# Experts sorted on the chip by token count, the last three with 64 slots and a stationary operand of heads and rests

## The chip, the cores and the metric

The kernel runs on one core of one Trainium2 chip. The metric is the device time of one execution in microseconds; several executions are timed, and their median is quoted. The core's engines are TensorE (PE, matrix products; its loads of the stationary operand are shown apart, as PEld), VectorE (DVE), ScalarE (ACT), GpSimd (POOL) and SyncE (SP, which only issues transfers here). They run side by side and meet through semaphores. Each runs its own instructions in the order in which they were laid down when the kernel was built.

## The reference

Two decoder layers on x of 256 tokens by 1024 channels, in float32. Each layer adds a mixer (gated DeltaNet heads, forgetting attention, pooling) and then a feed-forward: a dense SwiGLU in the first layer, and in the second the top 2 of 8 experts. The change lies in that last part:

```python
N_EXPERTS, TOP_K, D_FF_EXPERT = 8, 2, 1536

def moe_swiglu(h, router, w_gate, w_up, w_down):
    probs = jax.nn.softmax(ht @ router, axis=-1)          # ht: [256, 1024]
    top_p, top_i = lax.top_k(probs, TOP_K)
    top_p = top_p / jnp.sum(top_p, axis=-1, keepdims=True)
    gates = jnp.sum(one_hot(top_i, N_EXPERTS) * top_p[..., None], axis=1)
    for e in range(N_EXPERTS):
        out = out + gates[:, e:e + 1] * swiglu(ht, w_gate[e], w_up[e], w_down[e])

def swiglu(h, w_gate, w_up, w_down):
    return (jax.nn.silu(h @ w_gate) * (h @ w_up)) @ w_down
```

With the inputs of this case the router gives experts 0 to 7 the token counts 58, 74, 57, 74, 68, 67, 62 and 52 (256 tokens, two experts each).

## The kernel before

Four phases follow one another: mixer 0, the dense feed-forward, mixer 1, and "all", the experts. Float32 products are made of reduced ones: each operand is split into a head (hi) and a rest (lo = value - hi), and three products hi hi + hi lo + lo hi are summed in PSUM (`mm3`, L240 and on; all products are recorded at the line of `mm`, L236).

The weights stream from HBM in pieces of 128 rows by at most 1152 columns, into a ring of 6 buffers, 12 in the experts' phase (`load`, L260; SP issues all of them, at L266). `piece` (L269) splits each: ACT copies the head into `whi` (recorded at L230), DVE subtracts, `wlo = raw - whi` (recorded at L233). There are four buffers of whi and four of wlo. Pieces have a high priority, so that they run ahead of the work around them.

`route` (L963) computes logits, the softmax, the two best experts, and each token's slot at its experts (`pos`). `experts` (L1063) then takes the eight experts in order of their numbers, each with 128 slots, each in four chunks of 384 hidden channels, 32 steps in all:

- `gather` (L1066), for two experts at a time: 32 products with a one-hot matrix (`disp`, filled by DVE at L1041) put the chosen tokens into `ghi` and `glo`, channels on partitions.
- `gate_up` (L1083): six pieces (1152, 1152 and 768 columns for the gate, the same for the up product). The tokens are the stationary operand and the weights are the moving one, 384 columns; 16 row tiles by three products make 48 matmuls into `ps_e`. ACT then makes `esg` (SiLU), and DVE multiplies `ehh = up * esg`.
- `down` (L1101), one step later: three transposes of `ehh` into `ps_ht`, a split into `ehi` and `elo`, and three pieces of 1024 columns. Three pieces by two halves by three products make 18 matmuls of 512 columns into `ps_y`.
- `finish` (L1115) scales and splits the result (`yh`, `yl`) and builds the one-hot `Q`; `scatter` (L1126), after every second expert, adds the rows back to `xs` with 16 matmuls (`ps_sc`) and four DVE additions.

A step has 9 pieces, 288 in the phase. The order in which instructions stand on each engine comes from a scheduler that plays the program through with its own estimates; the kernel sets only priorities. At the end the output is stored, and if an expert had more than 128 tokens, a second pass (L1193) does the rest.

Of the kernel before, what the change touches and what calls it, by code (L numbers as in the profile page):

```python
# [35 lines left out]
NFC = 4  # L36
EPS = 1e-6
# [3 lines left out]
# column groups of w_in, in the order they are streamed: name, columns, channels on partitions or not  # L41
# [12 lines left out]
# row tiles of w_out in the order they are streamed  # L54
# [25 lines left out]
def shape_constants():  # L80
# [30 lines left out]
    r.add("lt", np.broadcast_to((e[None, :] < e[:, None]).reshape(1, 64), (128, 64)))  # L111
    return c, r
# [25 lines left out]
def pack(inputs):  # L138
    """Lays the inputs out in the order the chip reads them."""
# [42 lines left out]
class Kernel:  # L182
# [101 lines left out]
    def hi_lo(self, hi, lo, src, scale=None):  # L284
        """hi = float32r(src * scale), lo = src * scale - hi; scale is one value per partition."""
        if scale is None:
            return self.copy(hi, src), self.tt(lo, src, hi.bitcast(F32), ALU.subtract)
# [26 lines left out]
    def rsqrt(self, out, v, n):  # L314
        """out = v ** -0.5: exp(-ln(v) / 2) with one Newton step."""
# [9 lines left out]
    def gain(self, i):  # L325
        """The i-th norm's gain, on every partition."""
# [45 lines left out]
    def proj_tokens(self, g, hi, lo):  # L372
        """[token, channel] products; psum tiles for both token tiles."""
# [12 lines left out]
    def proj_channels(self, g, hi, lo):  # L386
        """[channel, token] products, one psum tile of 128 channels after the other."""
# [10 lines left out]
    def gates(self, ps):  # L398
        """Log decays, betas and everything that follows from them alone."""
# [11 lines left out]
        # softplus(zz) = max(zz, 0) + log1p(exp(-|zz|)); log1p(y) = ln(u) + (y - (u - 1)) / u, u = 1 + y  # L411
# [71 lines left out]
    def scaled(self, ps):  # L483
        """A product with channels on partitions, times the norm's factors."""
# [4 lines left out]
    def conv(self, g, m, ps, dest):  # L489
        """Causal convolution over tokens and SiLU, channels on partitions."""  # L490
# [20 lines left out]
    def silu(self, dest, x, eng):  # L511
        """x / (1 + exp(-x)) = x exp(-ln(1 + exp(-x))), in the table of the other functions."""
# [7 lines left out]
    def rnorm(self, src, scale, tag, ps=None):  # L520
        """(sum over a head's channels of src**2 * scale + eps) ** -0.5, for [channel, token]."""
# [19 lines left out]
        # 16-blocks by substitution, one 32-block of N per partition  # L541
# [21 lines left out]
        # the entries that join two 16-blocks  # L563
# [3 lines left out]
        # keys times exp(G), and keys with tokens on partitions times exp(G_last - G) beta  # L567
        # exp(G_t) along the free dimension, for every channel of a head
# [494 lines left out]
    def experts(self, base, xh, xl):  # L1063
# [78 lines left out]
        for i in range(len(steps) + 1):  # L1142
            cur = None
            if i < len(steps):
                e, fc = steps[i]
                if i == 0:
# [4 lines left out]
                    if not base:  # L1151
                        self.gates_of_experts()
# [74 lines left out]
```

## Time and profile before

| | |
|---|---|
| runs | 1006.22, 1005.40, 1004.65 us; median 1005.4 us |
| profiled execution | 1006.0 us, of which the span of the page is all |
| busy over the span | PE 95%, PEld 86%, DVE 74%, ACT 64%, POOL 13% |
| chain that ended last | PE 81%, POOL 6%, DVE 6%, ACT 3%, DMA 2%, issue 2% |
| read from HBM | 222.48 MB, 222 GB/s over the span |

The busy shares are of the whole span; phases differ. The chain is followed back from the last instruction, at each step to whatever released it. Matmuls are pipelined: the duration of one is longer than its distance to the next, so rates are read from runs of them. DVE and ACT instructions overlap by a little in the same way.

### The profile page before, as it was taken

Reading aid. Unit: us, or ns where it says so; the run is one execution under the profiler, and the core shown is the slowest. Engines: PE = TensorE matmul, PEld = TensorE weight load, DVE = VectorE, ACT = ScalarE, POOL = GpSimd, SP = SyncE. Lnnn points to the kernel's source line nnn. Section 1 sums busy time; section 2 is a strip of 40 time slices with the busy share of each in tenths; the row PEclk is TensorE's granted clock in tenths of the full one; section 3 lists DMA queues with packets and bytes.
Section 4 is the critical chain, followed back from the end, with each engine's and each line's share of the span. In section 5 each row is a group of like instructions: output and inputs, shape, how many; then the busy total and the mean of one; then the engine's idle time right before and its main releaser. Section 6 shows DMA issues by size and latency. Waiting matters only on the chain.

```text
span 1006.0 us, 17495 instructions
## 1 busy us (share of the span) xinstructions
PE 955.4 (95%) x6715; PEld 868.7 (86%) x6715; DVE 746.9 (74%) x1013; ACT 642.4 (64%) x969; POOL 130.6 (13%) x196
## 2 busy tenths in 40 slices
PE   6988998999999989899985999999999999999997
PEld 6987877999999979888765999998999899998995
DVE  5876657655555578776566789888997899888995
ACT  6754646544444458556454688876888688886873
POOL 2596000000000024970002000000000000000000
PEclk9998999999999999999997999999999999999999
DMA  9534114666666545241162799998999899998981
GB/s 347 161 92 124 44 43 132 214 187 186 188 188 180 164 150 181 85 136 56 40 234 73 245 363 369 364 309 301 367 371 321 282 358 367 355 317 301 368 327 45
DMA packets 61979, 224.75 MB, mean 223 GB/s; under 512 B 6896, under 2 KB 7152, under 8 KB 61888
## 3 DMA queue, kind: packets, MB, share of 16 engines
q1 hardware_dynamic: 61344, 221.62, 64.2%
q0 software_dynamic: 544, 1.94, 0.6%
q8 instruction: 54, 0.88, 0.4%
q14 instruction: 37, 0.30, 0.1%
HBM read 222.48 MB, written 1.05 MB: 222 GB/s over the span
## 4 chain that ended last, share of the span: by engine, by line
PE 81%; POOL 6%; DVE 6%; ACT 3%; DMA 2%; issue 2%; SPq 0%; DVEq 0%; POOLq 0%; ACTq 0%
PE ps_e L236 26%; PE ps_y L236 13%; PE ps_gu L236 13%; PE ps_dn L236 6%; PE ps_out L236 4%; PE ps_fq L236 3%; DVE wlo L233 2%; PE ps_ga L236 2%; PE ps_zabf L236 2%; PE ps_o L236 1%; POOL cacc L500 1%; PE ps_p L236 1%; POOL U L562 1%; PE ps_ht L1104 1%; DVE cacc L504 1%
## 5 line engine op out<-in xcount | busy, mean ns | idle before, releaser
L233 DVE TENSOR_TENSOR wlo<-raw,whi 128x1024 fp32r<-128x1024 f32 (+3 forms) x418 | 501.0, 1223 | 133.8 <-ACT whi L230 130.4
L230 ACT ACTIVATE whi<-raw 128x1024 fp32r<-128x1024 f32 (+3 forms) x418 | 437.9, 1056 | 203.2 <-PE ps_e L236 57.9
L236 PE MATMUL ps_e<-wlo,ghi 128*128 128x384 f32 x512 | 173.1, 338 | 0.0
L236 PE MATMUL ps_e<-whi,glo 128*128 128x384 f32 x512 | 172.6, 338 | 0.0
L236 PE MATMUL ps_e<-whi,ghi 128*128 128x384 f32 x512 | 171.5, 340 | 0.0
L236 PE MATMUL ps_gu<-hThi,whi 128*128 128x256 f32 x352 | 99.8, 283 | 1.3 <-DVE hTlo L233 1.3
L236 PE MATMUL ps_gu<-hThi,wlo 128*128 128x256 f32 x352 | 99.4, 283 | 0.0
L236 PE MATMUL ps_gu<-hTlo,whi 128*128 128x256 f32 x352 | 99.4, 282 | 0.0
L236 PEld LDWEIGHTS ps_e<-wlo,ghi 128*128 128x128 f32 x512 | 97.2, 190 | 1.8
L236 PEld LDWEIGHTS ps_e<-whi,glo 128*128 128x128 f32 x512 | 97.0, 189 | 2.0
L236 PEld LDWEIGHTS ps_e<-whi,ghi 128*128 128x128 f32 x512 | 96.9, 190 | 0.9
L236 PE MATMUL ps_y<-wlo,ehi 128*128 128x512 f32 x192 | 75.5, 396 | 0.0
L236 PE MATMUL ps_y<-whi,elo 128*128 128x512 f32 x192 | 74.9, 396 | 0.0
L236 PEld LDWEIGHTS ps_gu<-hThi,whi 128*128 128x128 f32 x352 | 67.3, 191 | 2.5 <-DVE hTlo L233 1.5
L236 PEld LDWEIGHTS ps_gu<-hTlo,whi 128*128 128x128 f32 x352 | 67.3, 191 | 1.0
L236 PEld LDWEIGHTS ps_gu<-hThi,wlo 128*128 128x128 f32 x352 | 67.3, 191 | 0.0
L236 PE MATMUL ps_y<-whi,ehi 128*128 128x512 f32 x192 | 62.6, 397 | 1.7 <-ACT ehi L230 1.7
L236 PEld LDWEIGHTS ps_y<-whi,ehi 128*128 128x128 f32 x192 | 35.7, 188 | 8.6 <-ACT ehi L230 2.5
L236 PEld LDWEIGHTS ps_y<-wlo,ehi 128*128 128x128 f32 x192 | 36.1, 188 | 7.2
L236 PEld LDWEIGHTS ps_y<-whi,elo 128*128 128x128 f32 x192 | 35.8, 188 | 6.8 <-DVE elo L233 0.2
L236 PE MATMUL ps_dn<-whi,fhi 128*128 128x512 f32 x88 | 35.0, 398 | 0.0
L236 PE MATMUL ps_dn<-wlo,fhi 128*128 128x512 f32 x88 | 34.8, 396 | 0.0
(366 smaller groups left out, 1728.2 us busy)
## 6 DMA issues: line engine op xcount, KB each, us to landing
raw<-moe SPq DMA_DIRECT2D x128, 576.0 KB, 5.7
raw<-moe SPq DMA_DIRECT2D x96, 512.0 KB, 5.4
raw<-ffn SPq DMA_DIRECT2D x66, 512.0 KB, 3.6
raw<-moe SPq DMA_DIRECT2D x64, 384.0 KB, 5.4
raw<-win SPq DMA_DIRECT2D x34, 512.0 KB, 3.7
raw<-wout SPq DMA_DIRECT2D x16, 512.0 KB, 3.7
raw<-win SPq DMA_DIRECT2D x8, 402.0 KB, 5.1
raw<-win SPq DMA_DIRECT2D x4, 576.0 KB, 4.8
```

The lines of the kernel that those rows point to most:

```text
L230: return self.nc.scalar.activation(out, in_, AF.Copy, scale=scale)
L233: return self.nc.vector.tensor_tensor(out, a, b, op=op)
L236: self.nc.tensor.matmul(out, l, r, start=start, stop=stop)
L500: eng.tensor_scalar(acc, x, w[:, o + 3:o + 4], None, op0=ALU.mult)
L504: nc.vector.scalar_tensor_tensor(acc[:, j:], x[:, :T - j], wj, acc[:, j:], op0=ALU.mult, op1=ALU.add)
L562: nc.gpsimd.tensor_tensor(u, u, tv, op=ALU.subtract)
L1104: nc.tensor.transpose(ps[:, j * 128:j * 128 + 128], hh[:, j * 128:j * 128 + 128], self.ident)
```

## The change

Experts are given places. `places` sorts them by token count on DVE, most first (expert 0 always comes first, so that its weights can be streamed before the order is known), moves slots, gates and counts into that order, and SP reads the order into registers (`values_load_multi_w_load_instructions`); from the second place on, the address of each weight piece comes from such a register (`weights`). Gathers cover the places 0, 1-2, 3-4 and 5-7. The last three places have 64 slots: the stationary operand holds 64 columns of heads and 64 of rests, so two products (with whi and with wlo) take the place of three, and the two halves of the result are added, in `gate_up` by a copy on ACT and an addition on DVE for each of the two products. In `down` nothing is added: the halves go through `finish` as 128 rows, and the scatter sums them. In every `down`, small or not, the rest of the third piece is made by GpSimd instead of DVE. The second pass runs if one of the first five has more than 128 tokens or one of the last three more than 64.

```diff
+NL = 5
+    r.add("room", np.broadcast_to(np.where(e < NL, 0.0, 64.0), (128, 8)))
...
-    def piece(self, ap):
+    def piece(self, ap, eng=None):
...
-            parts = self.hi_lo(hi[:, :n], lo[:, :n], src)
+            parts = self.hi_lo(hi[:, :n], lo[:, :n], src, eng=eng)
...
+            return self.copy(hi, src), (eng or self.nc.vector).tensor_tensor(lo, src, hi.bitcast(F32), op=ALU.subtract)
...
+    def places(self):
+        nc.vector.tensor_copy(cnt, self.counts[:, 16:24])
+        nc.vector.tensor_copy(key, cnt)
+        nc.vector.memset(key[:, 0:1], 2.0 * T)
...
+        self.tt(c2, others, mine, ALU.is_equal)
+        self.tt(c1, others, mine, ALU.is_gt)
+        self.tt(c2, c2, self.rc("lt").rearrange("p (a b) -> p a b", b=NE), ALU.mult)
+        self.tt(c1, c1, c2, ALU.add)
+        nc.vector.tensor_reduce(place, c1, axis=AX.X, op=ALU.add)
...
+        nc.vector.tensor_copy(order, moved("orderf", self.rc("iota")[:, :NE]))
+        with self.tc.high_priority(offset=2 * AHEAD):
+            _, regs = nc.values_load_multi_w_load_instructions(order[0:1, 1:NE], engines=[mybir.EngineType.SP], min_val=0, max_val=NE - 1)
+        self.order = [0, *regs]
...
+        for o, v in ((by, self.pos), (gp, self.gate)):
+            self.tt(c4, at[:, None].to_broadcast([128, 2, NE, NE]), v[:, :, None, :].to_broadcast([128, 2, NE, NE]), ALU.mult)
+            nc.vector.tensor_reduce(o, c4, axis=AX.X, op=ALU.add)
...
+        groups = ((0, 2), (2, 4), (4, 6), (6, 8)) if over else ((0, 1), (1, 3), (3, NL), (NL, NE))
...
+        def gate_up(p, fc, g, e):
+            small = p >= nl
...
+                        if small:
+                            x = g[k // 4][:, k % 4, e]
+                            self.mm(ps[:, :384], x, wh[:, c], k == 0, False)
+                            self.mm(ps[:, :384], x, wl[:, c], False, k == 7)
+                        else:
+                            self.mm3(ps[:, :384], g[0][:, k, e], g[1][:, k, e], wh[:, c], wl[:, c], k == 0, k == 7)
...
+            if small:
+                for x, ps in zip((sg, hh), pgu):
+                    self.copy(x, ps[64:, :384])
+                    self.tt(x, ps[:64, :384], x, ALU.add)
+                ga, up = sg, hh
+            self.act(sg, ga, AF.Silu, scale=info[0][:r, p, 2:3])
+            self.tt(hh, up, sg, ALU.mult)
...
-                wh, wl = self.piece(self.d["moe"][e, fc, :, 2, j * D:(j + 1) * D])
+                wh, wl = self.piece(self.weights(p, fc, 2, j * D, j * D + D), nc.gpsimd if j == 2 else None)
...
+                    if small:
+                        x = h[:, j].rearrange("p i c -> p (i c)")
+                        self.mm(py[i], x, wh[:, c], first, False)
+                        self.mm(py[i], x, wl[:, c], False, last)
...
+                    fill(self.pos, *groups[0], 128)
+                    g[0] = gather(*groups[0])
+                    if not over:
+                        self.gates_of_experts()
+                        self.places()
+                    fill(self.pos, groups[0][1], nl, 128)
+                    if nl < NE:
+                        fill(self.pos, nl, NE, 64)
...
-                elif fc == NFC - 2 and e % 2 == 1 and e + 1 < NE:
-                    g[e // 2 + 1] = gather(e + 1)
+                elif fc == NFC - 2 and p + 1 < NE and of[p + 1] not in g:
+                    g[of[p + 1]] = gather(*groups[of[p + 1]])
...
+    def weights(self, p, fc, s, a, b):
+        e = self.order[p]
+        if p == 0:
+            return d[0, fc, :, s, a:b]
+        return d[bass.ds(e, 1), fc, :, s, a:b].rearrange("o p n -> (o p) n")
```

## Rows read from the trace of the kernel before

**Rows 1.** Stretches: length, PE, PEld, DVE, ACT, POOL busy; clock; DMA share; GB/s.

```profile
823.00:991.00 168.00, 167.07 (x898) 154.56 (x896) 149.53 (x149) 133.36 (x149) 0.00 (x0) 1.00 0.88 319
700.00:712.00 12.00, 12.00 (x67) 11.32 (x66) 10.80 (x11) 9.64 (x11) 0.00 (x0) 1.00 1.02 392
520.00:530.00 10.00, 6.60 (x40) 5.39 (x41) 7.23 (x14) 7.53 (x17) 0.00 (x0) 1.00 0.88 353
540.00:550.00 10.00, 7.80 (x36) 7.44 (x36) 5.66 (x20) 1.56 (x3) 0.00 (x0) 0.55 0.01 2
```

**Rows 2.** Chain in order of time, experts' phase: start, length, what.

```profile
545.75 1.28 PE ps_e L236 x4
547.03 0.85 PE ps_ga L236 x4
571.89 3.26 PE ps_y L236 x14
575.15 0.33 PE ps_ht L1104 x3
576.59 8.15 PE ps_e L236 x47
865.10 0.47 PE ps_ga L236 x4
```

**Rows 3.** The longest wait, 823 to 991 us: total, times, longest one.

```profile
ACT whi L230 <- PE ps_e L236: 20.6, 44, 2.7
```

**Rows 4.** DMA, 823 to 980 us: what was moved.

```profile
DMA packets 14689, 53.56 MB, mean 341 GB/s; under 512 B 1636, under 2 KB 1636, under 8 KB 14677
```

**Rows 5.** Timeline of DVE: start, length, what, how many.

```profile
639.24 2.22 DVE L233 TENSOR_TENSOR wlo<-raw,whi 128x1152 fp32r<-128x1152 f32 x2
822.23 4.62 DVE L233 TENSOR_TENSOR wlo<-raw,whi 128x1024 fp32r<-128x1024 f32 x4
```

**Rows 6.** Timeline, end of the phase: DVE's last weight splits, PE's last `ps_y`.

```profile
985.90 4.65 DVE L233 TENSOR_TENSOR wlo<-raw,whi 128x1024 fp32r<-128x1024 f32 x4
...
994.21 0.39 PE L236 MATMUL ps_y<-whi,elo 128*128 128x512 f32 x1
```

**Rows 7.** DVE groups by shape, 823 to 991 us: busy, mean ns, idle before.

```profile
L233 DVE TENSOR_TENSOR wlo<-raw,whi 128x1152 fp32r<-128x1152 f32 x48 | 64.1, 1354 | 6.3 <-ACT whi L230 5.9
L233 DVE TENSOR_TENSOR wlo<-raw,whi 128x1024 fp32r<-128x1024 f32 x40 | 48.5, 1222 | 6.9 <-ACT whi L230 6.4 <-DMA raw<-moe 0.5
L233 DVE TENSOR_TENSOR wlo<-raw,whi 128x768 fp32r<-128x768 f32 x24 | 22.9, 952 | 1.0 <-ACT whi L230 1.0
L233 DVE TENSOR_TENSOR elo<-ps_ht,ehi 128x384 fp32r<-128x384 f32 x13 | 7.2, 550 | 0.0
L233 DVE TENSOR_TENSOR ehh<-ps_e,esg 128x384 f32<-128x384 f32 x12 | 6.7, 556 | 4.2 <-PE ps_e L236 3.6 <-ACT whi L230 0.6
L290 DVE SCALAR_TENSOR_TENSOR yl<-ps_y,slot,yh 128x512 fp32r<-128x512 f32 x6 | 4.5, 746 | 0.0
L233 DVE TENSOR_TENSOR xs<-xs,ps_sc 128x512 f32<-128x512 f32 x4 | 2.7, 682 | 0.0
```

**Rows 8.** Timeline, norm and router: GpSimd's split of the tokens beside DVE.

```profile
532.24 5.21 POOL L1186 TENSOR_TENSOR xl<-xn,xh 128x1024 fp32r<-128x1024 f32 x2 [13.15 <-ACT nr L210]
...
532.88 2.30 DVE L233 TENSOR_TENSOR nt<-nv,nr 128x2 f32<-128x2 f32 x1
...
535.21 2.27 DVE L233 TENSOR_TENSOR nt<-nt,nr 128x2 f32<-128x2 f32 x1
```

**Rows 9.** Timeline, mixer 0: a DVE instruction with a PSUM operand beside GpSimd.

```profile
77.93 1.42 POOL L562 TENSOR_TENSOR U<-U,tmp 128x120 f32<-128x120 f32 x1
...
78.98 0.41 DVE L233 TENSOR_TENSOR px<-ps_fk,R 128x256 f32<-128x256 f32 x1
```

**Rows 10.** Timeline, router and first gather: one DVE comparison, SP's issues.

```profile
530.85 34.25 SPq L266 DMA_DIRECT2D raw<-moe  x8
...
540.24 0.29 DVE L233 TENSOR_TENSOR c<-c,c 128x128 f32<-128x128 f32 x1
```

More of the change, by code (lines that the diff above doesn't have):

```diff
@@ L282, in piece, with hi_lo @@
         return hi, lo
[L284 removed]
+    def hi_lo(self, hi, lo, src, scale=None, eng=None):
         if scale is None:
[L287 removed]
+            return self.copy(hi, src), (eng or self.nc.vector).tensor_tensor(lo, src, hi.bitcast(F32), op=ALU.subtract)
         else:
@@ L1026, in gates_of_experts @@
         self.tt(gate, gate, su[:, :, None].to_broadcast([128, 2, NE]), ALU.mult)
-        most = sm.tile([128, 1], F32, name="most", bufs=1)
-        nc.vector.tensor_reduce(most, self.counts[:, 16:24], axis=AX.X, op=ALU.max)
-        mosti = cp.tile([128, 1], I32, name="mosti")
-        nc.vector.tensor_copy(mosti, most)
-        self.gate, self.most = gate, mosti
-    def dispatch(self, base):
-        nc, wk = self.nc, self.wk
-        if base:
-            nc.vector.tensor_scalar(self.pos, self.pos, float(base), None, op0=ALU.subtract)
-        P = [wk.tile([128, NE, 128], F32R, tag="t4", name=f"disp{t}", bufs=self.n4) for t in range(2)]
-        def fill(a, b):
-            for t in range(2):
-                self.tt(P[t][:, a:b], self.rc("iota")[:, None, :128].to_broadcast([128, b - a, 128]),
-                            self.pos[:, t, a:b, None].to_broadcast([128, b - a, 128]), ALU.is_equal)
-        return P, fill
+        self.gate = gate
     def slots(self, P):
@@ L1061, in slots, with experts, fill, gather @@
         return sl, tk
-    def experts(self, base, xh, xl):
+    def experts(self, over, xh, xl):
         nc, wk = self.nc, self.wk
-        P, fill = self.dispatch(base)
-        def gather(e0):
-            gh = self.big.tile([128, 8, T], F32R, tag="Thi", name="ghi")
-            gl = self.big.tile([128, 8, T], F32R, tag="Tlo", name="glo")
-            for k in range(0, 8, 2):
-                for src, dest in ((xh, gh), (xl, gl)):
+        nl = NE if over else NL
+        groups = ((0, 2), (2, 4), (4, 6), (6, 8)) if over else ((0, 1), (1, 3), (3, NL), (NL, NE))
+        P = [wk.tile([128, NE, 128], F32R, tag="t4", name=f"disp{t}", bufs=self.n4) for t in range(2)]
+        def fill(pos, a, b, w):
+            for t in range(2):
+                self.tt(P[t][:, a:b].rearrange("p e (i c) -> p e i c", c=w),
+                        self.rc("iota")[:, None, None, :w].to_broadcast([128, b - a, 128 // w, w]),
+                        pos[:, t, a:b, None, None].to_broadcast([128, b - a, 128 // w, w]), ALU.is_equal)
+        def gather(a, b):
+            n, small = b - a, a >= nl
+            w = 64 * n if small else 128 * n
+            g = [self.big.tile([128, 4 if small else 8, n, 128], F32R, tag=x, name="g" + x) for x in ("Thi", "Tlo")]
+            kk = min(4, 512 // w)
+            for k in range(0, 8, kk):
+                for j, src in enumerate((xh, xl)):
@@ L1071, in gather @@
                     ps = self.psF("ps_ga")
-                    for i in range(2):
+                    for i in range(kk):
                         ks = slice((k + i) * 128, (k + i + 1) * 128)
                         for t in range(2):
-                            self.mm(ps[:, i * T:i * T + T], src[t][:, ks], P[t][:, e0:e0 + 2].rearrange("p e c -> p (e c)"), t == 0, t == 1)
-                    to = dest[:, k:k + 2].rearrange("p k t -> p (k t)")
-                    if e0 == 0 and dest is gl:
-                        nc.vector.tensor_copy(to, ps)
-                    else:
-                        self.copy(to, ps)
@@ L1085, in gate_up @@
+                    if a == 0 and j == 1:
+                        nc.vector.tensor_copy(to, got)
+                    else:
+                        self.copy(to, got)
+            return g
+        def gate_up(p, fc, g, e):
+            small = p >= nl
             pgu = []
             for s in range(2):
-                p = self.psD("ps_e")
+                ps = self.psD("ps_e")
                 for k0, k1 in k_cuts(384):
-                    wh, wl = self.piece(self.d["moe"][e, fc, :, s, k0 * 384:k1 * 384])
+                    wh, wl = self.piece(self.weights(p, fc, s, k0 * 384, k1 * 384))
@@ new lines, in gate_up @@
+            sg = wk.tile([128, 384], F32, tag="esg", name="esg", bufs=2)[:r]
+            hh = wk.tile([128, 384], F32, tag="ehh", name="ehh", bufs=2)[:r]
+            ga, up = pgu[0][:, :384], pgu[1][:, :384]
+            if small:
[5 more added lines that the diff above has]
+            self.tt(hh, up, sg, ALU.mult)
@@ L1102, in down @@
+            return hh
+        def down(p, fc, hh, py):
+            small = p >= nl
+            r = 64 if small else 128
             ps = self.psF("ps_ht")
             for j in range(3):
-                nc.tensor.transpose(ps[:, j * 128:j * 128 + 128], hh[:, j * 128:j * 128 + 128], self.ident)
-            h1 = wk.tile([128, 384], F32R, tag="ehi", name="ehi", bufs=2)
-            h2 = wk.tile([128, 384], F32R, tag="elo", name="elo", bufs=2)
-            self.hi_lo(h1, h2, ps[:, :384])
+                nc.tensor.transpose(ps[:, j * r:j * r + r], hh[:, j * 128:j * 128 + 128], self.ident[:r, :r])
+            if small:
+                h = wk.tile([128, 3, 2, 64], F32R, tag="ehi", name="ehi", bufs=2)
+                h1, h2 = h[:, :, 0], h[:, :, 1]
+            else:
+                h1 = wk.tile([128, 3, 128], F32R, tag="ehi", name="ehi", bufs=2)
+                h2 = wk.tile([128, 3, 128], F32R, tag="elo", name="elo", bufs=2)
+            self.hi_lo(h1, h2, ps[:, :3 * r].rearrange("p (j c) -> p j c", j=3))
@@ L1116, in finish @@
+        def finish(p, py):
             sl, tk = info
@@ L1137, in scatter @@
                     self.tt(x, x, ps, ALU.add)
-        steps = [(e, fc) for e in range(NE) for fc in range(NFC)]
+        steps = [(p, fc) for p in range(NE) for fc in range(NFC)]
+        of = {p: i for i, (a, b) in enumerate(groups) for p in range(a, b)}
         g, prev, parts = {}, None, []
+        if over:
+            for a, b, n in ((0, NL, 128), (NL, NE, 64)):
+                nc.vector.tensor_scalar(self.pos[:, :, a:b], self.pos[:, :, a:b], float(n), None, op0=ALU.subtract)
         for i in range(len(steps) + 1):
@@ L1188, in moe @@
         self.tables("silu_and_others")
-        self.experts(0, xh, xl)
+        self.experts(False, xh, xl)
         self.store()
-        rv = nc.values_load(self.most[0:1, 0:1], min_val=0, max_val=T)
+        rv = nc.values_load(self.most[0:1, 0:1], min_val=0, max_val=2 * T)
         with self.tc.If(rv > 128):
-            self.experts(128, xh, xl)
+            self.experts(True, xh, xl)
             self.store()
```

78 lines of the change are left out of this document (51 added, 27 removed).

## Prediction

> **What bounds the kernel now.** I read the busy time by stretches first. [...] So PE sets the pace, and DVE is the next in line, only 18.5 us behind. The chain of waits says the same: from 545 us on it runs through PE, one run of `ps_e` or `ps_y` after the other, 0.173 us for each matmul of 384 columns (8.15 / 47) and 0.233 for each of 512 (3.26 / 14) [rows 2]. A step is 48 x 0.173 + 18 x 0.233 + 0.33 for the transposes = 12.85 us. The list of waits confirms the direction: what ACT mostly waits for is PE giving back a split buffer, 20.6 us in this stretch [rows 3]. Whoever takes work from PE here must ask what DVE can still take.
>
> **PE, the aim of the change.** In the last three experts a step has 32 matmuls of 384 columns and 12 of 512: 32 x 0.173 + 12 x 0.233 + 0.3 = 8.6 us, 4.2 less. Over 12 steps PE loses 50 us, and the gather inside this stretch besides. The steps can't become that short, since 9 pieces still have to be transferred and split in each. The bytes give one floor: 53.56 MB were moved after 823 us [rows 4]; at 392 GB/s, seen over 12 us with the transfers fully busy [rows 1], that is 136.6 us.
>
> [...]
>
> **DVE, what limits next.** I count what DVE has to do from the first split of the sixth expert (the second of the run at 822.23, so 823.4) to the last (985.90 + 4.65 = 990.55): 167.2 us now [rows 5, 6]. Instructions in a run overlap: a pair of 1152 and 768 columns takes 2.22 us, not 1.354 + 0.952, so each costs its mean less 0.086 [rows 5, 7]. 111 pieces are split in the stretch; 13 of them (the third of each `down`, line L233 by `piece`) go to GpSimd:
> - 48 x 1.268 + 24 x 0.866 + 26 x 1.136 = 111.2 us of splits that stay on DVE.
> - 12 `ehh` x 0.47 = 5.6; 24 new additions, two a step, of the same 384 columns = 11.3; `elo`, now half as wide, 12 x 0.264 and one old 0.46 = 3.6 (1152 and 768 columns differ by 0.402, so 192 columns are 0.20). Six `yl` = 4.0, four `xs` = 2.4, three `Q` by the same price per column 0.8. Together 27.7.
>
> That is 138.9 us. The question is what GpSimd's 13 splits cost DVE. The only row of such an instruction is the split of the tokens, two of the same 1024 columns in 5.21 us; beside them two DVE instructions on two columns, with both operands in SBUF, took 2.30 and 2.27 us, each until GpSimd's was done [rows 8]. The weight splits also read both operands from SBUF. So each split on GpSimd shuts DVE's next split out for some 2.27 us, twice the 1.14 it took on DVE itself: 13 x 2.27 = 29.5. A DVE instruction that has one operand in PSUM is not held: `px` took 0.41 us wholly inside a GpSimd instruction [rows 9]. The additions, `ehh`, `elo`, `yl` and `xs` are of that kind. If none falls under a GpSimd split, DVE needs 138.9 + 29.5 = 168.4; if all do (26.9), 141.5.
>
> Which do? Follow a small step: the up product's last split (0.87), then the first split of `down` (1.14). PE needs 0.7 us more for the up product, ACT a copy (about 0.5, by DVE's price for these columns); so the second addition is ready some 2 to 2.7 us after that last piece's turn began, when DVE is at the second `down` piece. GpSimd takes the third as soon as that one is finished, and the addition and `ehh` (2 x 0.47 = 0.94 us) are due just then. I take 0.94 us of cover a step, 11.3 in all. Against it, DVE waits for PE before `ehh`, 4.2 us for 12 now [rows 7]; I keep that. So DVE runs 168.4 - 11.3 + 4.2 = 161.3 us instead of 167.2. Behind a waiting addition stand all later splits, and behind those PE.
>
> ACT gets 24 copies, by DVE's price some 11 us on 133 [rows 1], less in `ehi`: it stays under DVE.
>
> **The first five experts.** There PE keeps its 12.85 us a step. DVE has 4 x 1.268 + 2 x 0.866 + 2 x 1.136 + 2.27 + 0.47 + 0.46 = 12.3, so the port is covered, by 0.6 us a step. I take nothing; if buffers don't even it out, up to 0.25 a step or 5 us.
> A third gather now stands among them (places 5 to 7): 32 matmuls between 0.12 (256 columns) and 0.11 (the transposes of 128) [rows 2], +3.7 us. The first gather is half as wide: 16 of its matmuls at the lower clock may go from 0.21 to 0.11, the others gain nothing: 0 to -1.8, I take -1.2.
>
> **Order and addresses.** `places` adds 19 DVE instructions of at most 0.3 us [rows 10], under 6 us. They come after the first gather's own fill; DVE is busy only 5.7 of 10 us at 540 to 550 [rows 1], and four pieces are split ahead, so I take 0. Uncovered, the first `esg` and the splits behind it on ACT would be late by up to 6. SP stands at the register reads until the order is there, with all later loads behind it; but it issues eight loads in 34 us at that time [rows 10], and the ring is full. The registers are first used by the 37th piece. Again 0. A register address in each issue isn't shown by any row; 252 issues are off the path as long as they keep under 1.4 us, the distance of pieces (12.85 / 9). Between 0 and some 5 us.
>
> **The end.** After DVE's last split PE needs 4.05 us now (990.55 to 994.60, where it works off a backlog); afterwards four matmuls, 0.93 [rows 6]. GpSimd's longer last split is in the count. What follows PE's last `ps_y` is unchanged.
>
> **Sum.** The stretch begins at 823.4 + 3.7 - 1.2 = 825.9; DVE ends at 987.2, PE at 988.1 against 994.6: -6.5 us. The profiled execution took 1006.0, the median is 1005.4, so 0.6 less: **999 us**.
>
> **The rivals.**
> - *The port isn't covered* (slower). If DVE's next instruction is a split whenever GpSimd takes over, nothing falls under it: 172.6 us instead of 161.3, and PE ends 4.8 us later than now: 1010. With a wait of 1 us a step instead of 0.35, 1018. It decides from a cover below 4.8 us, 0.4 a step: less than one addition. For it: DVE works strictly in order, and 9 of its 13 instructions a step are held back. Against it: the additions come due at the right moment.
> - *GpSimd costs DVE little* (faster by more). Nearly all PSUM readers fall under its splits: 141.5 to 153.5 us, 979 to 991, middle 986. The floor by bytes lies below that. For it: 26.9 us of such work and 29.5 of splits; against it: `yl` and `xs` come in lumps, where no split of GpSimd is due.
> - *Order or addresses come late*: the reads or the register addresses hold the stream, up to 11 us by the bounds above: some 1005.
> [...]
> - *The second pass runs*: it would add nearly the phase, over 400 us. The counts (three smallest after expert 0: 52, 57, 62; most 74) exclude it.
>
> **How the numbers follow.** Forecast 0.47 (993 to 1005), port uncovered 0.28, little cost 0.16, late order or addresses 0.05, clock 0.04. The time is the forecast's, 999. Its neighbours lie on both sides, so the range takes most of both: 984 to 1015. A measurement can tell about 0.2%, 2 us, from no change. Faster takes the little-cost case and 0.37 of the forecast, 0.53; within 0.2% 0.07 of the forecast, 0.06 of the uncovered port and 0.03 of the late order, 0.16; slower the rest, 0.31.
>
> **What would show it.** In the last three experts: PE busy near two thirds and DVE near full, GpSimd's splits at 2.2 to 2.4 us when nothing precedes them, and single weight splits on DVE lengthened to 2 us and more behind them. Additions inside GpSimd's time speak for the cover; DVE standing before a split throughout speaks for the first rival. A step should last near 13.4 us there and 12.85 among the first five, and little should lie between DVE's last split and PE's last `ps_y`. Wrong would be: steps below 12.5 us, PE still at full load there, SP waiting for the order after 560 us, or a clock well under 1.00.

## The result and the profile after

The changed kernel takes 1013.8 us (median; 1013.34 to 1014.87), the kernel before 1005.8 beside it: a ratio of 1.0083, 95% interval 1.0068 to 1.0097. It is slower by 8 us, where 6.5 us less had been forecast. The profiled execution took 1013.9 us with a span of 1011.2; the span of before was 1006.0. So 5.2 us lie inside the span. Of the rest, executions of the kernel before measured with the experiments below show that it, too, takes 1.8 us outside its span (1007.76 for a span of 1006.0), against 2.7 here: 0.9 more, and some 2 us are the difference between one execution and a median. The forecast had taken the span of before for its whole time; its base was probably 1.8 us too low.

First the stretches: length, busy time of PE, PEld, DVE, ACT and POOL, granted clock, DMA share, GB/s. The first answers to the 823 to 991 us of [rows 1].

```profile
825.00:999.00 174.00, 144.50 (x630) 114.45 (x630) 163.75 (x159) 134.15 (x169) 33.61 (x14) 0.92 0.85 304
570.00:824.00 254.00, 252.68 (x1375) 234.78 (x1373) 220.09 (x204) 203.25 (x230) 44.66 (x19) 1.00 0.95 341
550.00:560.00 10.00, 10.00 (x53) 10.00 (x52) 3.25 (x6) 2.01 (x2) 0.00 (x0) 0.67 0.20 59
```

In the last three experts PE is no longer full (144.5 of 174 us, it was 167 of 168), DVE is: 163.8. The bound moved from PE to DVE, as meant, and the stretch got longer all the same. From the first split of the sixth expert (824.7) to the last split of all (998.3) it lasts 173.6 us; before it was 167.2, forecast were 161.3. The second row is the five large experts: PE full, DVE with 34 us to spare.

Next what DVE does from 824 to 999 us, by shape (busy, mean ns, idle before), against [rows 7]:

```profile
L291 DVE TENSOR_TENSOR wlo<-raw,whi 128x1152 fp32r<-128x1152 f32 x48 | 69.7, 1470 | 7.2 <-ACT whi L234 7.2
L291 DVE TENSOR_TENSOR wlo<-raw,whi 128x1024 fp32r<-128x1024 f32 x26 | 40.9, 1578 | 0.5 <-ACT whi L234 0.5
L291 DVE TENSOR_TENSOR wlo<-raw,whi 128x768 fp32r<-128x768 f32 x24 | 22.7, 945 | 0.0
L237 DVE TENSOR_TENSOR ehh<-ehh,esg 64x384 f32<-64x384 f32 x12 | 14.6, 1220 | 0.2
L237 DVE TENSOR_TENSOR esg<-ps_e,esg 64x384 f32<-64x384 f32 x12 | 6.5, 542 | 0.0
L237 DVE TENSOR_TENSOR ehh<-ps_e,ehh 64x384 f32<-64x384 f32 x12 | 6.5, 542 | 0.0
```

The mean of a split of 1024 columns rose from 1222 to 1578 ns, that of 1152 from 1354 to 1470. The line to look at is the fourth: the multiplication `ehh` went from 556 to 1220 ns in the mean, although it became half as tall: eight of the twelve took 0.54 us, four 2.5 to 2.6. The two additions, which read `ps_e` from PSUM, are at 542. The timeline shows why (start, length, what):

```profile
862.77 2.95 POOL L291 TENSOR_TENSOR wlo<-raw,whi 128x1024 fp32r<-128x1024 f32 x1 [11.12 <-ACT whi L234]
...
863.72 3.21 DVE L291 TENSOR_TENSOR wlo<-raw,whi 128x1152 fp32r<-128x1152 f32 x1 [0.25 <-ACT whi L234]
...
947.98 0.54 DVE L237 TENSOR_TENSOR ehh<-ps_e,ehh 64x384 f32<-64x384 f32 x1
...
948.39 2.36 POOL L291 TENSOR_TENSOR wlo<-raw,whi 128x1024 fp32r<-128x1024 f32 x1 [12.16 <-ACT whi L234]
...
948.56 2.60 DVE L237 TENSOR_TENSOR ehh<-ehh,esg 64x384 f32<-64x384 f32 x1
```

At 862.8 GpSimd splits a piece, and DVE's split beside it takes 3.21 us instead of 1.35. At 948.4 it is `ehh` that waits: after the addition both its operands, `ehh` and `esg`, lie in SBUF. It takes 2.60 us and ends 0.41 us after GpSimd's instruction (948.39 + 2.36 = 950.75; it ends at 951.16). The same holds for all of GpSimd's thirteen splits here but the last, when DVE has nothing left to do: one DVE instruction beside each is long, and ends 0.4 to 1.3 us after it.

The end of the phase, against [rows 6]: the last split is GpSimd's and ends at 998.32, PE's last `ps_y` at 999.40.

```profile
995.90 2.42 POOL L291 TENSOR_TENSOR wlo<-raw,whi 128x1024 fp32r<-128x1024 f32 x1 [3.31 <-ACT whi L234]
...
998.79 0.61 PE L240 MATMUL ps_y<-wlo,ehi 128*128 128x512 f32 x2
```

Who waits for whom, 825 to 999 us (total, times, longest): PE hardly waits for GpSimd itself, but for the held `ehh`, and ACT's copy of the next transposes then waits for PE.

```profile
PE ps_y L240 <- POOL wlo L291: 1.1, 2, 0.7
PE ps_ht L1176 <- DVE ehh L237: 7.9, 4, 2.0
ACT ehi L234 <- PE ps_ht L1176: 10.6, 5, 2.5
```

### The profile page after: what moved, and what is told of

Its sections match the earlier page's. It is cut to its first block, busy times and chain, and to the rows that moved or that the text cites. A ratio compares the mean times of both kernels' runs of the same rounds, so it can differ in the third digit from the quotient of the medians.

```text
span 1011.2 us, 17588 instructions
## 1 busy us (share of the span) xinstructions
PE 929.9 (92%) x6451; PEld 825.3 (82%) x6451; DVE 760.2 (75%) x1024; ACT 644.0 (64%) x991; POOL 210.0 (21%) x228
## 4 chain that ended last, share of the span: by engine, by line
PE 64%; DVE 15%; DMA 7%; POOL 6%; ACT 4%; issue 3%; SPq 0%; DVEq 0%; ACTq 0%; POOLq 0%
PE ps_e L240 17%; PE ps_gu L240 13%; DVE wlo L291 8%; PE ps_y L240 7%; PE ps_dn L240 6%; DMA raw<-moe 5%; PE ps_out L240 4%; PE ps_fq L240 2%; ACT whi L234 2%; PE ps_ga L240 2%; PE ps_o L240 1%; POOL cacc L504 1%; PE ps_p L240 1%; DVE ehh L237 1%; DVE cacc L508 1%
## 5 line engine op out<-in xcount | busy, mean ns | idle before, releaser
L291 POOL TENSOR_TENSOR wlo<-raw,whi 128x1024 fp32r<-128x1024 f32 x32 | 79.3, 2477 | 383.2 <-ACT whi L234 282.0
L240 PE MATMUL ps_e<-wlo,gThi 128*128 128x384 f32 x416 | 147.9, 355 | 9.4 <-DVE wlo L291 8.7
L240 PE MATMUL ps_e<-whi,gThi 128*128 128x384 f32 x416 | 145.1, 352 | 1.3 <-ACT whi L234 1.2
L240 PE MATMUL ps_e<-whi,gTlo 128*128 128x384 f32 x416 | 141.6, 341 | 0.0
L240 PEld LDWEIGHTS ps_e<-wlo,gThi 128*128 128x128 f32 x416 | 81.7, 196 | 21.3 <-DVE wlo L291 19.4
L240 PEld LDWEIGHTS ps_e<-whi,gThi 128*128 128x128 f32 x416 | 81.6, 196 | 4.8 <-ACT whi L234 2.9
L240 PEld LDWEIGHTS ps_e<-whi,gTlo 128*128 128x128 f32 x416 | 79.9, 192 | 1.5
L240 PE MATMUL ps_y<-whi,elo 128*128 128x512 f32 x120 | 46.2, 393 | 0.0
```

Source lines behind the costliest of these rows:

```text
L240: self.nc.tensor.matmul(out, l, r, start=start, stop=stop)
L291: return self.copy(hi, src), (eng or self.nc.vector).tensor_tensor(lo, src, hi.bitcast(F32), op=ALU.subtract)
```

## The experiments

The theories: **P**, GpSimd's splits hold those instructions of DVE that read two operands from SBUF. **R1**, PE waits for GpSimd's own 2.4 us. **R2**, the copies and additions make the small experts slow by themselves. **R3**, the order and the register addresses cost it. Later ones (R4 to R6, H1, H2) are told where they come up. Each edit is against the changed kernel unless another is named, and is shown abridged; ratios are to the kernel before on the same chip, which had medians of 1006.85, 1006.63 and 1006.02 us in the three groups of runs.

**All splits on DVE.**

```diff
-wh, wl = self.piece(self.weights(p, fc, 2, j * D, j * D + D), nc.gpsimd if j == 2 else None)
+wh, wl = self.piece(self.weights(p, fc, 2, j * D, j * D + D))
```

> All splits of the weights go back to DVE; the rest of the change stays. Theory P (two-SBUF-operand work of DVE is held while GpSimd splits, and `ehh` of the small experts is such work): DVE's run from the first split of the sixth expert to the last split was 173.6 us in the changed kernel, of which 15.4 us lie in lengthened splits and 12 x (1.22 - 0.54) = 8.2 us in lengthened `ehh`. Both go, 13 splits x 1.22 = 15.9 us come back, and some 4 of the 7.6 us of idle time: a run of about 162 us, the kernel 1000 to 1004 us, below the kernel before. Rival R1 (GpSimd's own 2.4 us per split is what PE waits for, DVE is not held): also faster, but every split of DVE is as long as before and the run is not a DVE-bound one. Rival R2 (the copies, the additions and their waits in DVE's order make the small experts slow by themselves): 1010 us or more. Rival R3 (order and register addresses): within 2 us of 1013.8.

Measured: 1003.64 us, ratio 0.9966 (0.9953 to 0.9979). Without GpSimd the change is a small gain. The stretch of the small experts, first in one row, then DVE's work in it:

```profile
826.00:985.00 159.00, 131.73 (x617) 104.53 (x615) 153.93 (x172) 134.65 (x169) 0.00 (x0) 0.98 0.89 334
```
```profile
L291 DVE TENSOR_TENSOR wlo<-raw,whi 128x1152 fp32r<-128x1152 f32 x48 | 64.3, 1353 | 2.7 <-ACT whi L234 2.7
L291 DVE TENSOR_TENSOR wlo<-raw,whi 128x1024 fp32r<-128x1024 f32 x40 | 47.8, 1222 | 0.1
...
L237 DVE TENSOR_TENSOR ehh<-ehh,esg 64x384 f32<-64x384 f32 x12 | 6.7, 556 | 0.0
```

Every length is that of before again, `ehh` at 556 ns with the same two operands in SBUF. DVE's run is 158.3 us (826.3 to 984.6) with 153.9 of work in it, though it splits 13 pieces more. R2 and R3 as causes of the loss fall.

**The same splits on DVE, and GpSimd working for nobody.**

```diff
+if scrap:   # third piece of each down, last three experts
+    o = self.wk.tile([128, 960], BF16, tag="scrap", name="scrap", bufs=1)
+    self.nc.gpsimd.tensor_tensor(o, src[:, :960], hi[:, :960].bitcast(F32), op=ALU.subtract)
```

> As the run with all splits on DVE, and besides, for the third piece of each `down` of the last three experts (12 in all) GpSimd does a subtraction of the same two operands (960 of 1024 columns) into a scrap tile that nobody reads: no work waits for GpSimd, only its presence is added. P: about 12 x 2 us of hold less what falls under PSUM-side work: 10 to 20 us slower than the run with all splits on DVE, 1012 to 1022 us, with DVE splits of 2.5 to 3.5 us beside GpSimd's. R1: the same time as the run with all splits on DVE, within 2 us, and no lengthened split.

Measured: 1027.36 us, ratio 1.0200 (1.0181 to 1.0220), 23.7 us more than without the scrap. Nothing reads its result, so R1 can't explain this. Two of the twelve in the timeline, with DVE beside the first:

```profile
850.67 2.29 POOL L283 TENSOR_TENSOR scrap<-raw,whi 128x960 bf16<-128x960 f32 x1 [312.31 <-ACT whi L234]
864.30 6.47 POOL L283 TENSOR_TENSOR scrap<-raw,whi 128x960 bf16<-128x960 f32 x1 [11.34 <-ACT whi L234]
...
850.66 0.55 DVE L237 TENSOR_TENSOR esg<-ps_e,esg 64x384 f32<-64x384 f32 x1
851.12 5.33 DVE L294 TENSOR_TENSOR wlo<-raw,whi 128x1024 fp32r<-128x1024 f32 x3
```

The addition at 850.66 isn't touched; three splits behind it take 5.33 us together. Without GpSimd three of these shapes cost 1.14 to 1.27 each (the run prices of the prediction), some 3.5. P holds; the price is even above the 10 to 20 us that it asked for.

One thing does wait for the scrap: it reads `raw` and `whi`, so ACT gets these buffers back later (the first line: who waited for it, us, times). That this makes the kernel slower is a rival, and the trace speaks against it: over the stretch (second line) DVE is busy 174.4 of 180 us and so idle 5.6, where it was idle 5.1 without the scrap. DVE doesn't stand still more, its instructions are longer: twelve of them, 20.6 us in all, read one by one.

```profile
  ACT whi L234: 15.8, 7
827.00:1007.00 180.00, 139.50 (x615) 113.00 (x614) 174.42 (x172) 135.43 (x168) 59.32 (x12) 0.91 0.81 294
```

So far the rows show two kinds. In the changed kernel DVE instructions with both operands in SBUF took 3.21 us (a split, 1.35 without GpSimd) and 2.60 us (`ehh`, else 0.54) beside GpSimd's; here an addition with one of its two operands in PSUM took 0.55 us (at 850.66). One kind of instruction with a single tensor from SBUF was held too, the one-hot `Q` where it came next to a GpSimd subtraction: one of the two here took 1.28 us, where both took 0.36 without the scrap.

```profile
L1207 DVE TENSOR_SCALAR Q<-rcst,slott 128x256 fp32r<-128x256 f32 x2 | 1.6, 808 | 0.0
```

**The same, but GpSimd copies one operand.** In the same order of instructions on every engine.

```diff
-    self.nc.gpsimd.tensor_tensor(o, src[:, :960], hi[:, :960].bitcast(F32), op=ALU.subtract)
+    self.nc.gpsimd.tensor_copy(o, src[:, :960])
```

> As the run with GpSimd's unused subtraction (1027.4 us), in the same order of instructions on every engine, but GpSimd does a copy with one operand in SBUF (960 columns) into the scrap tile. If any access of GpSimd to SBUF holds DVE (P, wide): slower than the run with all splits on DVE by GpSimd's time, 1010 to 1027 us. If only the two-operand work of GpSimd holds it (P, narrow): 1001 to 1006 us and no lengthened split.

Measured: 1008.2 us (1005.1 to 1011.2), ratio 1.0020 (1.0003 to 1.0037). That is 4.6 us over the run without any (5.4 by the ratios), about a fifth of what the subtraction cost, and neither of the two expected values: one operand held DVE too, but far less. Read one by one, eleven DVE instructions are longer than without the copies, by 6.3 us in all against 20.6 beside the subtractions. All twelve copies, then all twelve subtractions of the run above (duration in ns: least, median, most):

```profile
L283 POOL CAST scrap<-raw x12: 1621/3350/7926, 838.3 to 976.8; 128x960 bf16<-128x960 f32 x12
```
```profile
L283 POOL TENSOR_TENSOR scrap<-raw,whi x12: 2292/5364/6943, 850.7 to 1001.5; 128x960 bf16<-128x960 f32 x12
```

**The multiplication reads PSUM.** The additions write in place, so `ehh` has one operand in PSUM as in the large experts.

```diff
-self.tt(x, ps[:64, :384], x, ALU.add)
+self.tt(ps[:64, :384], ps[:64, :384], x, ALU.add)
-ga, up = sg, hh
+ga, up = ga[:64], up[:64]
```

> The two additions of the small experts are written in place in PSUM, so that Silu and the multiplication `ehh` read PSUM as in the first five experts; GpSimd keeps its splits. P: the 12 `ehh` are back at 0.54 us (8.2 us less) and their share of a GpSimd split is covered; 4 to 8 us faster than the changed kernel, 1006 to 1010 us; the 5 `ehh` of 2.5 us are gone. R1 and R2: 1013 us or more (the bank of `ps_e` is released later). R3: 1013.8.

Measured: 1013.3 us (1010.4, 1011.2, 1015.4, 1015.5), ratio 1.0070 (1.0042 to 1.0097). By the median nothing is gained over the changed kernel. The profiled execution is the lowest of the four, with a stretch of 168.5 us, and there `ehh` is indeed free:

```profile
L291 DVE TENSOR_TENSOR wlo<-raw,whi 128x1152 fp32r<-128x1152 f32 x48 | 74.4, 1567 | 6.3 <-ACT whi L234 6.3
L291 DVE TENSOR_TENSOR wlo<-raw,whi 128x1024 fp32r<-128x1024 f32 x26 | 42.4, 1639 | 0.5 <-ACT whi L234 0.5
...
L237 DVE TENSOR_TENSOR ehh<-ps_e,esg 64x384 f32<-64x384 f32 x12 | 6.5, 544 | 0.2
```

But the splits are longer than in the changed kernel (74.4 + 42.4 against 69.7 + 40.9, 6.2 us), which eats most of the 8.1 that `ehh` gave back. The expectation fell: the hold isn't a property of `ehh`. With `ehh` at 544 ns in the mean the splits paid it, 1567 and 1639 ns where they took 1470 and 1578 in the changed kernel. Why the four executions lie 5 us apart wasn't found out.

**The order as constants.**

```diff
-self.order = [0, *regs]
+self.order = [0, 1, 3, 4, 5, 6, 2, 7]      # and plain addresses in weights(), no register reads
```

> The order of the experts is written as constants (the order that these inputs give), so that SP reads no registers and the addresses of the weights are fixed; the sort itself and the moved positions stay. R3: the time outside the span falls from 2.7 to 0.3 us and the gathers' start is as before, 1008 to 1011 us. P: the span stays at 1011 within 2 us; it says nothing on the time outside the span.

Measured: 1016.47 us, ratio 1.0091 (1.0072 to 1.0110); with registers it was 1.0083. The time outside the span is 2.6 to 3.0 us, as with registers. R3 falls on both counts. P had the span within 2 us of 1011; it is 1012.7 to 1014.2, so a little longer. The 0.9 us outside the span stay unexplained: they are there in this run, the one before it and the changed kernel, and not in the others, some of which have GpSimd's splits too.

**GpSimd for the large experts only.**

```diff
-nc.gpsimd if j == 2 else None
+nc.gpsimd if j == 2 and not small else None
```

> GpSimd keeps the third split of each `down` in the first five experts and gives it back to DVE in the last three, where DVE sets the pace. P: a GpSimd split costs only where DVE has no idle time; in the first five experts DVE idles 34 of 254 us, so the time is that of the run with all splits on DVE, 1003.6 us, within 3 us, and DVE's run of the small experts is 158 us again. Rival R4 (GpSimd's splits cost the same everywhere): 20 x 0.8 us more, 1015 us or more.

Measured: 1005.08 us, ratio 0.9983 (0.9968 to 0.9998), 1.4 us over the run with all on DVE (1.7 by the ratios), for 20 splits: 0.07 us each, within the error. R4 falls. The row of the large experts shows the room DVE has there:

```profile
570.00:824.00 254.00, 252.70 (x1375) 234.91 (x1374) 220.34 (x204) 203.25 (x231) 44.26 (x18) 1.00 0.94 341
```

**Three products everywhere, all splits on DVE.** The sort stays, the last three experts have 128 slots.

```diff
-NL = 5
+NL = 8
-groups = ... else ((0, 1), (1, 3), (3, NL), (NL, NE))
+groups = ... else ((0, 1), (1, 3), (3, 5), (5, 7), (7, 8))
```

> All splits on DVE, the sort kept, and the last three experts worked as the first five: 128 slots, three products, no copies and additions (the gathers are of 1, 2, 2, 2 and 1 experts). P: what two products give or take by themselves is the difference to the run with all splits on DVE (1003.6 us). With three products PE needs 12.85 us a step against DVE's counted 12.3: the small experts' run is back near 167 us, the kernel 1006 to 1012 us. R2 (two products give nothing, because of what they add to DVE): 1000 to 1004 us.

Measured: 1012.24 us, ratio 1.0052 (1.0037 to 1.0068). So with DVE doing all splits two products instead of three are worth 8.6 us (1.0052 - 0.9966), and the sort with its gathers costs 5.2. Both figures hold the fifth gather that this run has and the two others, with four, don't: an estimated 3.5 us of PE (32 matmuls of 128 columns at 0.11), since it falls where PE is full. PE is the bound again:

```profile
826.00:995.00 169.00, 168.08 (x914) 156.37 (x913) 148.97 (x149) 133.17 (x150) 0.00 (x0) 1.00 0.87 313
```

**The additions moved to PE.** If DVE's work sets the small experts' run, taking the additions away must shorten it. ACT copies all 128 rows of both products, and PE adds the halves while it transposes.

```diff
+fold = ident[:, :64] + ident[:, 64:]          # once
+self.copy(sg, ga, info[0][:, p, 2:3]); self.copy(hh, up)      # 128x384 each
+for i in range(6):
+    self.mm(ps[:, i * 64:i * 64 + 64], hh[i // 3][:, i % 3 * 128:i % 3 * 128 + 128], fold)
+self.act(s, ps[:, :192], AF.Silu)
+self.tt(s, ps[:, 192:384], s, ALU.mult)        # then the split of s; all weight splits on DVE
```

> All splits on DVE, and the two additions leave DVE: ACT copies both products with all 128 rows (the gate's with its scale), PE adds head and rest rows while it transposes (six products with a stationary 128x64 pair of identities in place of three transposes), and Silu, the multiplication and the split work on 128x192. DVE's 154 us of work in the small experts lose 36 x 0.55 and gain 12 x 0.35: 138 us. P (DVE's work sets the run): the run falls from 158 us toward the next limit, the weight stream: 12 steps of 4.72 MB at the 400 GB/s that its best 10-us slices show, 142 us; with waits 146 to 152 us, the kernel 990 to 998 us. Rival R5 (PE's late stretches and its clock set it already): 1001 us or more.

Measured: 989.76 us (988.89 to 990.15), ratio 0.9830 (0.9798 to 0.9861): faster than both kernels, and just below the expected range. The stretch is 148.1 us (827.6 to 975.7). Its row, and one of 10 us inside it:

```profile
827.00:976.00 149.00, 139.78 (x744) 121.68 (x743) 141.89 (x149) 130.02 (x171) 0.00 (x0) 0.99 0.92 357
860.00:870.00 10.00, 9.85 (x57) 8.57 (x55) 10.00 (x11) 10.00 (x14) 0.00 (x0) 1.00 1.03 411
```

DVE's work fell from 153.9 to 141.9 us and the time with it; R5 falls. In the second row all is full at once: PE 9.85, DVE and ACT 10 of 10, the transfers above 1. What is left is shared by everyone.

**The same with GpSimd's third split again**, in all eight experts (the line of the first diff put back).

> The folded version (989.8 us with all splits on DVE) with the change's third split of each `down` on GpSimd again, in all eight experts. From the runs so far a GpSimd split costs DVE's run 31.2 / 13 = 2.4 us in the changed kernel (its whole duration) and takes 1.22 us from DVE. P: 12 to 13 x 1.2 us slower than the folded version, 1003 to 1007 us, in the small experts alone. Rival R6 (with DVE relieved of the additions the weight stream sets the pace, and DVE has room for the hold): within 4 us of 989.8.

Measured: 1001.93 us, ratio 0.9960 (0.9944 to 0.9975), 12.2 us more than without (13.1 by the ratios), at or a little under the lower end of the expected 13 to 17. R6 falls. Here the price has two halves. The stretch (162.2 us) and DVE's waits in it:

```profile
825.00:987.00 162.00, 144.86 (x737) 121.23 (x736) 140.60 (x135) 130.78 (x169) 35.73 (x14) 0.98 0.87 327
```
```profile
DVE wlo L291 <- ACT whi L234: 11.4, 13, 1.6
DVE ehs L237 <- ACT ehs L214: 7.1, 5, 2.0
```

DVE's busy time is the same as without GpSimd (140.6 against 141.9) although it has 13 splits less, 15.9 us: so some 15 us of hold (12.9 read one by one, ten splits of 1152 columns, one of 1024 and one `Q`). And it stands idle 21 us instead of 7, most of that before work of ACT; that ACT is late because of the hold is likely, but wasn't tried apart.

**The start of the phase.** In the changed kernel the first expert ends at 619.7, before at 615.2, and the sort with its gathers had cost 5.2 us. One part needs no experiment: the second gather now stands in the first expert, while before it stood in the second. Its first matmuls, after and before:

```profile
588.82 0.72 PE L240 MATMUL ps_ga<-disp,xh 128*128 128x256 f32 x4
640.72 0.72 PE L236 MATMUL ps_ga<-disp,xh 128*128 128x256 f32 x4
```

By the prediction's 0.12 us a matmul that moves 3.7 us of PE's time into the first expert. Two theories on the rest: **H1**, DVE's sort chain delays the first gather's copies; **H2**, PE runs longer at its lower clock (granted 0.50). Three runs, the first two against the folded version with all splits on DVE:

```diff
+w = self.psD("ps_warm")                       # in route, after ps_lg; nobody reads it
+for i in range(56):
+    self.dep(self.nc.tensor.matmul(w[:, :T], hi[:, i % 8, :128], hi[:, i % 8], start=i == 0, stop=i == 55), last)
```

> The folded version with all splits on DVE, and 56 products of 128x256 that nobody reads (about 6 us of PE at the higher clock) in the 8 us in which PE waits for the routing's `sel` before the first gather. In the folded version's trace PE begins the first gather at 544.2 at the lower clock (the granted clock is 0.5 there) and runs at it until some 560; in the kernel before the full clock was back at 549.2, and the first expert ended 6 to 7 us earlier. Theory H2 (the late start of the first expert in the changed kernel is PE's clock): the first expert ends 4 to 8 us earlier, the kernel 982 to 986 us. Rival H1 (it is DVE's sort chain in front of the gather's copies): the first expert's end moves by under 2 us, 988 to 991 us.

```diff
-key ... place ... at ... moved(...)            # DVE's sort, register reads
+for i, j, m in ((0, 0, 2), (2, 3, 4), (6, 2, 1), (7, 7, 1)):
+    nc.vector.tensor_copy(o[:, :, i:i + m], v[:, :, j:j + m])     # slots, gates, counts
```

> The folded version with all splits on DVE, the order of the experts written as constants: no keys, comparisons and products with the permutation on DVE, twelve small copies instead, no register reads and fixed addresses. H1 (the sort chain delays the first expert): 3 to 6 us faster, 984 to 987 us. H2 (PE's clock, with the first gather of one expert): within 2 us of 989.8, with the first expert's end within 2 us of the folded version's 622.6.

The third is the kernel before with the 56 products.

> The kernel before with the same 56 unread products in the same wait. H2: the kernel before loses less at its first gather (clock 0.55 from 542.4 to 549.2, that is about 7 us at half rate), so it gains 2 to 4 us, 1002 to 1005 us, less than the folded version gains from the same. H1: 1005 to 1007 us.

Measured: 984.61 us with the products (ratio 0.9798, 0.9778 to 0.9818), 5.2 less than without them; 989.05 without the sort (0.9831, 0.9811 to 0.9851), 0.7 less. The folded version ran on another chip than these two: by the ratios the gains are 3.2 us and none. On their own chip the two are 4.4 us apart. So H2 and not H1, for the changed head. PE's timeline of the folded version, then with the products (a view from 533 us on, which holds 48 of the 56):

```profile
544.68 1.70 PE L240 MATMUL ps_ga<-disp,xh 128*128 128x128 f32 x7
...
549.80 0.52 PE L240 MATMUL ps_e<-wlo,gThi 128*128 128x384 f32 x1
...
562.26 0.52 PE L240 MATMUL ps_e<-whi,gThi 128*128 128x384 f32 x1
562.58 0.39 PE L240 MATMUL ps_e<-wlo,gThi 128*128 128x384 f32 x1
```
```profile
532.70 7.04 PE L989 MATMUL ps_warm<-hThi 128*128 128x256 f32 x48
...
541.18 0.96 PE L240 MATMUL ps_ga<-disp,xh 128*128 128x128 f32 x7
...
544.00 0.34 PE L240 MATMUL ps_e<-wlo,gThi 128*128 128x384 f32 x1
```

```profile
540.00:550.00 10.00, 6.06 (x31) 6.00 (x31) 8.83 (x45) 2.95 (x7) 0.00 (x0) 0.50 0.01 2
540.00:550.00 10.00, 9.08 (x68) 9.06 (x68) 8.92 (x35) 3.21 (x4) 0.00 (x0) 1.00 0.00 0
```

A matmul of 384 columns lasts 0.52 us at a granted clock of 0.50 and 0.34 at 1.00 (540 to 550 us, the two rows above: 0.50 without the products, 1.00 with them). Without the products PE is at the lower clock at the gather and again as late as 562 (0.50 from 560 to 562 us). With them the first expert ends 5.3 us earlier, counted from the phase's own first split (614.0 - 520.7 against 622.6 - 524.0).

The kernel before, though, has 1005.63 us with the products (0.9990, 0.9974 to 1.0005): 0.4 less, within the error, where H2 had 2 to 4. Its trace shows where the gain went in part:

```profile
533.71 8.36 PE L985 MATMUL ps_warm<-hThi 128*128 128x256 f32 x56
```

The products last until 542.07, and the first gather begins at 543.2 instead of 542.4. From there to the end of the first expert it takes 70.2 us instead of 72.8, so the clock (granted 1.00 from 540 to 550 us, where it was 0.55) cost 2.6 us here, as H2 had it, of which 0.8 are lost again. In the folded version the same distance went from 78.4 to 73.1, in the changed kernel it is 79.0. So of the 6.2 us between the kernel before (72.8) and the changed one, an estimated 2.7 are the clock (5.3 less 2.6, if the changed kernel loses what the folded version does), and the 3.5 that are left fit the gather that moved (3.7). Why the median of the kernel before gains 0.4 and not 1.8 us isn't settled; the interval allows it.

## Why the prediction was wrong

**The bound and its successor** were right: PE gives way, DVE is next, the small experts stop being PE's (rows of the first fence). The 999 us fell over one term, DVE's run of the last three experts, 161.3 forecast and 173.6 measured. Step by step:

- *DVE's own work, 138.9 us.* Right. With 13 splits of 1.22 us (15.9) back it would be 154.8; with all splits on DVE 153.9 were measured. In the changed kernel it is 140.5: 164.0 us busy over the run, less 23.5 of lengthening.
- *GpSimd's splits, 29.5 less 11.3 of cover, 18.2 us.* This step failed, and in the cover. Read one by one, 13 DVE instructions (nine splits, four `ehh`) are longer than without GpSimd, by 1.2 to 2.1 us each and 23.5 in all (one of them by a split of GpSimd begun before the run). With the 2.2 us that GpSimd's last split lasts after DVE's that makes 25.7. The 13 splits took 32.6 us instead of 29.5 (2.36 to 2.95 each; the first row counts 33.6, with the end of one begun before), and 3.7 us of that, not 11.3, fell beside DVE instructions that read PSUM: 0.3 us a step instead of 0.94. Half of the forecast cover was `ehh`, which was put among the PSUM readers from [rows 7], where it reads `ps_e`; the diff writes the sum to SBUF first, so it is itself held. The other half was the second addition. It lies mostly ahead of GpSimd's split, as at 947.98 above, or comes after it; the first addition lies beside it in five steps. The mistake on `ehh` alone isn't the cause: with `ehh` reading PSUM the median stayed.
- *Waits, 4.2 us.* Also too low: DVE is idle 7.3 us. The forecast kept its wait for PE before `ehh` and put the 14.2 us at nothing that it stood before its splits in [rows 7], mostly for ACT's `whi`, without giving a reason. About half of those remain (7.2 and 0.5 us in the first two DVE rows of after), while the wait before `ehh` fell to 0.2. ACT in turn waits for PE, and PE for the held `ehh` (7.9 us).
- Together: +1.6, +7.5 and +3.1 are the 12.3 us but for rounding.
- *The rival "the port isn't covered"* had 172.6 us of run and PE's end 4.8 us later; measured 173.6 and 4.8 (999.4 against 994.6). Its account, that DVE's next split is held and nothing lies under it, is the one that the runs confirm by the lengths (13 instructions, 23.5 us longer in all); no view shows a port. Its condition held: a cover below 4.8 us, and 3.7 were measured. That its figure is so close is partly luck, for its hold was too long (29.5 us against 25.7) and its work and waits too short (143.1 against 147.8). What it was given too little of is the chance.
- *A reading of [rows 9]:* `px` runs from 78.98 to 79.39 us and GpSimd's instruction only to 79.35, so it doesn't lie wholly inside. What was taken from it, that a DVE instruction with a PSUM operand is not held, is borne out by `esg` at 850.66 (0.55 us, 0.552 in the mean without GpSimd).
- *First five experts, 0.* Right: 1.4 us with GpSimd's splits there alone.
- *Third gather +3.7, first gather -1.2.* The sum, first split of the sixth expert at 825.9, was near (824.7). Counted from the phase's first split (521.1, before 522.5) the shift is +2.7 us where +2.5 was forecast. Its parts weren't right. A gather half as wide saved nothing at the lower clock (granted 0.50 in both): seven matmuls of 128 columns take 1.70 us, one every 0.21, and before three of 256 took 0.84, one every 0.21 as well:

```profile
541.20 1.70 PE L240 MATMUL ps_ga<-disp,xh 128*128 128x128 f32 x7
543.00 0.84 PE L236 MATMUL ps_ga<-disp,xh 128*128 128x256 f32 x3
```

  And PE's clock came back later (0.67 in 550 to 560 us, where it was 0.96 before). With the gather that moved the first expert so ended 4.5 us late. Most of that was back by the sixth expert; where some 2 us of it came from isn't shown.
- *Order and addresses, 0.* Right within 1 us: at most 0.7 for the sort, no gain without registers, although SP stood 11.2 us before the register reads.
- *PE's clock*, 0.04 of the chances: no run shows as a case of its own what a lower clock would cost there. Measured were 0.92 in the stretch, with 0.83 from 850 to 860 us and 0.50 from 910 to 915. PE, busy 144.5 of 174 us, had room for it.
- *The end*, 0.93 us from last split to last `ps_y`: 1.1 (998.3 to 999.4).

What the change as a whole came to, from the ratios: two products -8.6 us, the sort and its gathers +5.2 (both contain the fifth gather of the run with three products, an estimated 3.5 us), GpSimd's splits +11.8 (1.0083 - 0.9966), nearly all of it in the three small experts.

## What to carry to other kernels

Before work goes from DVE to GpSimd, list for each DVE instruction that can run beside it where its two operands lie after the edit, and price GpSimd's whole duration against the work taken off: here 2.5 us on GpSimd for 1.2 on DVE, a loss where DVE set the pace and next to none where PE did (1.4 us for twenty splits). Don't count on cover: here 13 DVE instructions came out 23.5 us longer and PE waited 7.9 us for the held `ehh`; with `ehh` reading PSUM the splits paid in its place. When the aim is to shorten the next engine's work, look for an engine with room; here PE could add two halves while it transposed, which, with all splits back on DVE, turned +8 us into -17.

## What was new about the hardware

- GpSimd's instruction is lengthened as well. The same subtraction took between 2.29 and 6.94 us, twelve of them 59.3 in all. The one at 864.30 lasted 6.47 us; three splits of DVE beside it kept their usual 1.21 to 1.35 us, and only the split after the addition `ehh<-ps_e,ehh` at 868.25 was held (3.27 us). From that addition to GpSimd's end it is 2.5 us, little more than the shortest of the twelve. In eleven of the twelve the instruction just before the held one reads PSUM, as `esg` at 850.66 does. From these lengths alone the author's reading is that GpSimd got in beside such an instruction, though not beside every one, and got nowhere before that; no view shows what it waited for.
- A GpSimd copy with one operand in SBUF held DVE too (6.3 us in eleven instructions), but twelve cost 4.6 us against 23.7 for twelve subtractions of the same columns.
- At a granted clock of 0.50 a matmul of 128 columns came every 0.21 us, no faster than one of 256; at 1.00 it was 0.11 (six intervals in 0.96 - 0.29 us).
